# Nested self-attention on one core: zeroes for V from GpSimd, and a 64-row projection order for the 448-row pair

## The chip, the cores and the metric

The kernel runs on one core of a Trainium2 chip. The metric is the device time of one execution, in microseconds (us). Three runs of the kernel before gave 341.05, 342.54 and 338.79 us, a median of 341.05. The engines are written as in the profile: PE (TensorE matmul), PEld (TensorE weight load), DVE (VectorE), ACT (ScalarE), POOL (GpSimd), SP (SyncE).

## What is computed

Thirty-two sequences of up to 512 rows and 512 columns (8 heads of 64) go through a fused projection and softmax attention; each sequence uses only its first `lengths[b]` rows, and all other output rows are zero.

```
for b in range(batch):
    x_b = x[b, :lengths[b]]
    q, k, v = split(x_b @ w_qkv)            # 8 heads of 64 each
    attn = softmax(q @ k.T / sqrt(64))      # per head
    output[b, :lengths[b]] = attn @ v
```

The draw is fixed. Sorted by length, the sequences are worked in 16 pairs, and each pair has a class N, its longer length rounded up to a multiple of 32 (340 is one more class):

| pair | lengths | class | tiles of 128 rows |
|---|---|---|---|
| 0 | 502, 447 | 512 | 4 |
| 1 | 446, 436 | 448 | 4 |
| 2, 3, 4 | 363, 357; 351, 347; 343, 333 | 384, 352, 352 | 3 |
| 5, 6, 7 | 323, 315; 310, 261; 260, 257 | 340, 320, 288 | 3 |
| 8, 9, 10 | 246, 230; 223, 220; 216, 183 | 256, 224, 224 | 2 |
| 11, 12, 13 | 164, 152; 143, 140; 134, 119 | 192, 160, 160 | 2 |
| 14, 15 | 101, 86; 79, 75 | 128, 96 | 1 |

## The kernel before

The program holds, for each class, one straight piece of code per engine and jumps between the pieces by the class read at run time (graph, L1140). A piece has two halves, h = 0 and h = 1, one per sequence of the pair. Half h does the attention of sequence h while it projects Q, K and V of the next sequence, g = 1 - h, whose width W is N, or the next lower class where the pair is the last of its class (leave, L1100). Tensors are doubled by h: xT (transposed input), qkT, v_aug (V with a 65th column of ones per head) and onat (output).

The order on PE is written by hand as a string of tokens (ORDER, L671, and DENSE, L676), read in half (L682):

- S: scores of one head pair for one key tile, two matmuls of 64 contraction rows, into s0 or s1; ACT takes the exponential into ep (L346) and so frees the bank. For dense classes (3 tiles, N up to 340) D does a whole head pair.
- Q, K: a projection of one head pair, four matmuls of 128 rows. Lower case gives its copy to ACT (L409), upper case to DVE (L410). E begins Q and K of a head pair at once in two banks, as eight matmuls of 64 rows; F, G, H or I ends them in eight more, and says which engine copies which bank (G: the first DVE, the second ACT). U and W do the same for two tiles of V.
- V: one tile of V, copied with the row mask by DVE (L433). If the last tile has at most 64 rows (half_rows, L510: W of 288, 320, 160, 192), vsides (L515) computes its two column halves on two halves of the partitions; DVE then writes the low columns (L529), clears the upper partitions of the high columns (L530) and writes their lower partitions (L531).
- A: probabilities times V, 65 columns a matmul; DVE takes the reciprocal (L610) and multiplies into onat (L629, L631). A leading + spreads A's matmuls between those of the step before it (spread_last, L655).
- O: ACT issues the store of the first half of onat; SP stores the second.

Banks: three-tile classes go through four banks in turns (a0, a1 in pa; v0, v1 in pav; in_turns, L842), and an A takes one bank. Two- and four-tile classes alternate a0 and a1 for projections, and A takes pav whole.

POOL's loop (L1699) waits in each half for s_vf, which the first score matmuls of the half raise when v_aug of g may be overwritten; it writes the column of ones (L1652, raising s_on), waits for s_x16f, and casts the input of a later sequence to 16 bit (L1647), after which SP issues the next load and, in the following half, the transposes. PE waits for s_on of h before the half's first A (L754; L698 in one-tile halves).

Of the kernel before, what the change touches and what calls it, by code (L numbers as in the profile page):

```python
# [13 lines left out]
P = 128  # L14
NH = 8
HD = 64
NPAIR = 4
# [6 lines left out]
SECOND = {4: 20, 3: AGAIN, 2: 0, 1: None}  # L24
AT_DENSE = 20
FIRST_DENSE = 4
PIECE = 266
PIECE_DENSE = 274
DENSE_ROWS = 340
# [121 lines left out]
def kernel(  # L151
# [363 lines left out]
    def vsides(pr, b, h, t):  # L515

        n = D // 2
        mms = [
            mm(area[b][HD * a : HD * (a + 1), 0:n], xT[h][:, c, t * P : t * P + HD],
               w_r[:, c, 2 * D + a * n : 2 * D + (a + 1) * n], c == 0, c == NC - 1)  # L520
            for c in range(NC)
            for a in range(2)
        ]

        def evac(e):
            keep = now[0][:, 0, t : t + 1].unsqueeze(2)
            low, high = v_aug[h][:, t, 0:NPAIR, 0:HD], v_aug[h][:, t, NPAIR:NH, 0:HD]
            src = area[b][:, 0:n].rearrange("p (a d) -> p a d", d=HD)
            e.tensor_tensor(out=low, in0=src, in1=keep.broadcast_to([P, NPAIR, HD]), op=ALU.mult)  # L529
            e.memset(high[HD:P], 0.0)  # L530
            return e.tensor_tensor(  # L531
                out=high[0:HD], in0=src[HD:P],
                in1=keep[0:HD].broadcast_to([HD, NPAIR, HD]), op=ALU.mult,
            )

        acquire(pr, b)
        close(pr, b, "dve", mms, True)
        evacuate(pr, b, "dve", evac)
# [5 lines left out]
            return  # L544
        group(pr, b, "dve", v_mms(b, h, i, T, of), v_out(b, h, i, T, of))

    def attnv(pr, h, i, T, late=False, b=None):

        for s_ in ("s0", "s1"):
            if pr.pair[s_] == i or T == 1 and pr.pair[s_] is not None:  # L550
                acquire(pr, s_)
        for v in halves_av if b is None else (b,):
            acquire(pr, v)
        va = v_aug[h]
        if b is not None:
            jobs = [(2 * 74 * qt, i, qt) for qt in range(T)]
        elif T == 1:
            jobs = [(74 * 2 * j, j, 0) for j in range(NPAIR)]
        elif T == 4:
            jobs = [(256 * qt, i, qt) for qt in range(T)]  # L560
        else:
            jobs = [(74 * (4 * qt + 2 * (i % 2)), i, qt) for qt in range(T)]
        mms = []
        for o0, j, qt in jobs:
            for par in range(2):
                o = o0 + par * (HD + 1 if T == 4 else 74)
                into = pav if b is None else area[b]
                for kt in range(T):
                    mms.append(
                        mm(  # L570
                            into[:, o : o + HD + 1],
                            ep[:, j, par, kt, qt * P : (qt + 1) * P],
                            va[:, kt, 2 * j + par, :],
                            kt == 0,
                            kt == T - 1,
                        )
                    )
        if b is None and T in (2, 3) and i % 2 == 0:
            acquire_carry(pr, mms)
            return  # L580
        on = onat[h]
        if b is not None:
            res = into[:, 0 : 2 * 74 * T].rearrange("p (t a d) -> p t a d", a=2, d=74)
            dst = on[:, i // 2, 0:T, P * (i % 2) : P * (i % 2 + 1)]
            dst = dst.rearrange("p t (a d) -> p t a d", d=HD)
            sh, fin = [T, 2], i % 2 == 1
        elif T == 4:
            res = pav.rearrange("p (j n) -> p j n", n=256)[:, :, 0 : 2 * (HD + 1)]
            res = res.rearrange("p j (a d) -> p j a d", d=HD + 1)
            dst = on[:, i // 2, :, P * (i % 2) : P * (i % 2 + 1)]  # L590
            dst = dst.rearrange("p t (a d) -> p t a d", d=HD)
            sh, fin = [NT, 2], i % 2 == 1
        else:
            sh, fin = [2, 4] if T == 1 else [T, 4], True
            res = pav[:, 0 : 74 * sh[0] * 4].rearrange("p (b j d) -> p b j d", j=4, d=74)
            if T == 1:
                dst = on[:, :, 0, :].rearrange("p b (j d) -> p b j d", d=HD)
            else:
                dst = on[:, i // 2, 0:T, :].rearrange("p t (a d) -> p t a d", d=HD)
        rv = rcp[:, i, 0 : sh[0] * sh[1]].rearrange("p (j a) -> p j a", a=sh[1])  # L600
        num, den = res[..., 0:HD], res[..., HD]
        name = "av" if b is None else b
        close(pr, name, "dve", mms, False)
        each = T == 4 or b is not None

        def recip():
            for j in (0, 1) if T == 1 else (i // 2,) if not each or i % 2 == 0 else ():
                pr.take("dve", s_od[h][j], 16)
            pr.take("dve", full[(name, "dve")])
            pr.add("dve", lambda e: e.reciprocal(out=rv, in_=den).then_inc(s_r, 1))  # L610

        def mult():
            pr.take("dve", s_r)

            if T == 1:
                cuts = [(slice(0, 2), 0)]
            elif h == 0:
                cuts = [(slice(0, T - 1), None), (slice(T - 1, T), T - 1)]
            else:
# [26 lines left out]
        if not late:  # L646
            for fn in todo.values():
                fn()
        return todo
# [25 lines left out]
    }  # L675
    DENSE = "K2 q2 D E1 E3 I1 H3 D k0 c A0 Q0~ A1 D V2 O V1 A2 D A3~ V0"  # L676

    def read_class(pr, h):
        for g in ("act", "dve") if h == 0 else ("pe",):
# [2 lines left out]
    def half(pr, h, T, N, W, st, last=False):  # L682
# [11 lines left out]
        if T == 1:  # L694
            start_proj()
            qk(pr, "a0", g, [(i, 0) for i in range(NPAIR)], W, P)
            qk(pr, "a1", g, [(i, 1) for i in range(NPAIR)], W, P, "act")
            pr.take("pe", s_on[h])  # L698
            attnv(pr, h, 0, 1)
            vwhole(pr, g)  # L700
            read_class(pr, h)
            for b in ("a0", "a1"):
                acquire(pr, b)
            pr.signals.append(s_xtf[g])
            if last:
                act_store(pr, h, 0, T)
            scores(pr, h, g, 0, 0, 1, W)
# [2 lines left out]
            return  # L710
        per = T if T >= 3 else 1
        units = [(i, k) for i in (1, 2, 3, 0) for k in range(per)]
        first, norm, dones, both = True, {}, 0, []
        dense, turns = is_dense(N), in_turns(N)
        toks = (DENSE if dense else ORDER[T]).split()

        def pick(second=False):
            if turns:
# [11 lines left out]
        for tok in toks:  # L730
# [16 lines left out]
            elif k == "D":  # L747
                i = units[0][0]
                del units[:T]
                scores_dense(pr, *((g, i, W) if i == 0 else (h, i, N)))  # L750
            elif k == "A":
                if first:
                    first = False
                    pr.take("pe", s_on[h])  # L754
                b = pick(over2) if turns else None
                if turns:
                    assert len(st["seen"]) == len(area), st["seen"]
                    for v in area:
                        if st["holds"].get(v) == (h, "V"):
                            acquire(pr, v)  # L760
                norm[i] = attnv(pr, h, i, T, f"X{i}" in toks, b)
                if turns:
                    give(b)
                if over:
# [5 lines left out]
            else:  # L770
# [26 lines left out]
                else:  # L797
                    bs = (pick(over2),)
                if k == "V":
                    vtile(pr, bs[0], g, i, tiles, T, W)  # L800
                elif k in "Bb":
                    qk(pr, bs[0], g, [(i, 0), (i, 1)], W, 256, eng)
# [37 lines left out]
        return -(-N // P) == 3 and 3 * N <= 2 * MAXS  # L840

    def in_turns(N):  # L842
        return -(-N // P) == 3 and (not is_dense(N) or "E" in DENSE)

    def make_body(N, W, last=False):

# [44 lines left out]
    def make_prologue():  # L891
# [143 lines left out]
        for tok in "Q2 K2 S0 S1 Q3 K3 V0 S2 S3 V1 X2 V2 X3 V3".split():  # L1035
# [23 lines left out]
                cast_second(3)  # L1059
            bank ^= 1  # L1060
        pr.add("dve", mask_table)
        return pr

    def class_table(e):
# [75 lines left out]
    def graph(e, name, opening=None, before=None):  # L1140
# [13 lines left out]
        def align(N, slots, off=0):  # L1154
# [2 lines left out]
                slot = AT_DENSE  # L1157
            elif slots is FIRST and is_dense(N):
                slot = FIRST_DENSE
            if fetch and slot is not None:  # L1160
                e.addr_align(FETCH, offset=(slot + off) % FETCH, max_nops=0)

# [158 lines left out]
    with nc.Block() as block:  # L1321
# [295 lines left out]
        def _(e):  # L1617
# [30 lines left out]
                    s_xc[h], 1  # L1648
                )

            def ones(h, T, src):
                e.tensor_copy(  # L1652
                    out=v_aug[h][:, 0:T, :, HD],
                    in_=src[:, 0, 0:T].unsqueeze(2).broadcast_to([P, T, NH]),
# [44 lines left out]
            def body(e, N):  # L1699
                T = -(-N // P)  # L1700
                for h in range(2):
                    wait_dec(e, s_vf[1 - h])
                    rv = e.snap(rank, min_val=0, max_val=B - 1)
                    ones(1 - h, T, masks[:, bass.ds(rv, 1), :, :].rearrange(
                        "p o a t -> p (o a) t"))
                    wait_dec(e, s_x16f[1 - h])
                    cast(1 - h, T)
                    if T == 1:
# [104 lines left out]
```

## Time and profile before

| | |
|---|---|
| runs | 338.79, 341.05, 342.54 us |
| profiled execution | 339.78 us |
| its span, first to last instruction | 338.0 us |
| granted TensorE clock | 0.996 |
| pair of class 448 | from 63.41 to 99.67 us |
| twelve 3-tile halves | from there to about 237 us |
| twelve 2-tile halves | about 237 to 316 us |

A group row reads: line, engine, operation, output<-input, shapes, count | busy us, mean ns of one | idle time before, and what ended it. A timeline row reads: start, us, engine, line, operation, count, and in brackets the idle time before it with its releaser. A row of several instructions covers them from the first start to the last end; matmul ends are modelled, so the step from one start to the next is the better measure of what PE spends. A wait row reads: engine, what waited, for what, us in total, times, longest (one kind has two engine rows, PE and PEld). L59 is the semaphore take and L304 the matmul helper, so PE's rows are told apart by their tiles.

### The profile page before, as it was taken

What the parts mean: (1) busy time and instruction counts of PE and PEld (TensorE: products, weight loads), DVE (VectorE), ACT (ScalarE), POOL (GpSimd) and SP (SyncE); (2) the same over time, 40 slices, a digit from 0 to 9 for tenths busy, and PEclk for the clock granted to TensorE, in tenths of its full rate; (3) what the DMA queues carried; (4) which work ended last, traced back from release to release, by engine and by line L of the source; (5) the groups of instructions that cost most, each with busy time, mean ns of one, the idle gap of its engine ahead of it and who ended that gap; (6) DMA issues with size and microseconds to landing.
All of it is one profiled execution on the core that took longest, in us unless ns stands there. A gap on an engine that the chain in (4) does not pass through costs nothing. (4 is left out here: it accounts for less than half of the span.)

```text
span 338.0 us, 12174 instructions
## 1 busy us (share of the span) xinstructions
PE 324.0 (96%) x4326; PEld 207.2 (61%) x4327; DVE 215.3 (64%) x580; ACT 240.0 (71%) x337; POOL 63.2 (19%) x102
## 2 busy tenths in 40 slices
PE   7899999999999999999999999999999999999991
PEld 2565544555545656556666676777677777676770
DVE  3576566666665576567567556765767667777672
ACT  4567887777769878877977887778775666555541
POOL 3634020202010210220220122012111211221340
PEclk9999999999999999999999999999999999999998
DMA  6956799966856976986787978697899657886732
GB/s 203 360 145 215 131 395 243 355 155 214 163 183 153 299 263 162 282 294 183 233 305 247 225 237 298 137 260 218 209 148 240 189 148 170 200 166 154 174 105 69
DMA packets 82273, 72.11 MB, mean 213 GB/s; under 512 B 40652, under 2 KB 63180, under 8 KB 82196
## 3 DMA queue, kind: packets, MB, share of 16 engines
q1 hardware_dynamic: 70340, 59.61, 66.7%
q10 hardware_dynamic: 11856, 11.54, 9.8%
q8 instruction: 40, 0.66, 0.8%
q14 instruction: 37, 0.30, 0.4%
HBM read 25.32 MB, written 36.70 MB: 183 GB/s over the span
## 5 line engine op out<-in xcount | busy, mean ns | idle before, releaser
L346 ACT ACTIVATE ep<-psc 128x704 f16<-128x704 f32 (+7 forms) x193 | 156.8, 858 | 60.2 <-PE psc L304 42.9
L304 PE MATMUL pa<-xT,w_r 128*128 128x224 f16 (+21 forms) x984 | 134.0, 276 | 3.0 <-PEq L59 1.3
L304 PEld LDWEIGHTS pa<-xT,w_r 128*128 128x128 f16 (+1 forms) x984 | 74.7, 97 | 35.5 <-issue 14.1
L410 DVE CAST qkT<-pa 128x448 f16<-128x448 f32 (+9 forms) x85 | 48.7, 574 | 47.1 <-PE pa L304 46.0
L304 PE MATMUL psc<-qkT 64*128 64x352 f16 (+17 forms) x702 | 66.9, 287 | 0.9 <-PEq L59 0.3
L304 PE MATMUL pa<-w_r,xT 128*128 128x512 f16 (+4 forms) x356 | 63.4, 333 | 0.6 <-DVE v_aug L531 0.5
L304 PE MATMUL pav<-v_aug,ep 128*128 128x65 f16 x1414 | 62.1, 194 | 0.2 <-PEq L59 0.2
L304 PEld LDWEIGHTS pav<-v_aug,ep 128*128 128x128 f16 x1414 | 55.4, 98 | 9.7 <-issue 1.4
L1652 POOL CAST v_aug<-masks 128x24 f16 (+4 forms) x33 | 9.1, 276 | 245.4 <-POOLq L1281 245.4
L631 DVE SCALAR_TENSOR_TENSOR onat<-pav,masks,rcp 128x128 f32<-128x128 f32 (+2 forms) x137 | 48.2, 391 | 5.6 <-DVE rcp L610 2.1
L378 ACT ACTIVATE ep<-psc 128x960 f16<-128x960 f32 (+3 forms) x48 | 43.3, 960 | 8.8 <-PE psc L304 6.0
L433 DVE TENSOR_TENSOR v_aug<-pa,masks 128x512 f16<-128x512 f32 (+1 forms) x52 | 34.8, 675 | 14.7 <-PE pa L304 13.8
L304 PE MATMUL pav<-xT,w_r 64*128 64x352 f16 (+10 forms) x328 | 43.6, 300 | 0.3 <-DVE v_aug L433 0.3
L1647 POOL CAST x<-x_nat 128x1536 f16<-128x1536 f32 (+3 forms) x33 | 42.0, 1274 | 9.2 <-POOLq L1281 8.4
L304 PEld LDWEIGHTS psc<-qkT 64*128 64x128 f16 x702 | 25.8, 94 | 29.0 <-issue 20.6
L304 PEld LDWEIGHTS pa<-w_r,xT 128*128 128x128 f16 (+2 forms) x356 | 24.9, 98 | 21.0 <-issue 4.8
L409 ACT CAST qkT<-pa 128x352 f16<-128x352 f32 (+7 forms) x58 | 26.4, 461 | 15.0 <-PE pa L304 8.0
L304 PEld LDWEIGHTS pav<-xT,w_r 64*128 64x128 f16 (+1 forms) x328 | 23.7, 95 | 10.0 <-issue 2.1
L610 DVE RECIPROCAL rcp<-pav 128x8 f32<-128x8 f32 (+1 forms) x71 | 14.0, 198 | 20.4 <-PE pav L304 15.7
L304 PE MATMUL pav<-w_r,xT 128*128 128x512 f16 (+3 forms) x100 | 19.3, 343 | 0.0
L304 PEld LDWEIGHTS pa<-v_aug,ep 128*128 128x128 f16 x378 | 13.5, 98 | 4.3 <-issue 1.8
L629 DVE TENSOR_TENSOR onat<-pav,rcp 128x256 f32<-128x256 f32 (+1 forms) x32 | 14.6, 457 | 1.1
(84 smaller groups left out, 146.4 us busy)
## 6 DMA issues: line engine op xcount, KB each, us to landing
out_dram<-zt SPq DMA_DIRECT2D x16, 768.0 KB, 6.1
x_nat<-in_x_dram SPq DMA_DIRECT2D x12, 512.0 KB
x_nat<-in_x_dram SPq DMA_DIRECT2D x5, 1024.0 KB
out_dram<-onat ACTq DMA_DIRECT2D x12, 384.0 KB, 5.4
out_dram<-onat SPq DMA_DIRECT2D x12, 384.0 KB, 4.7
x_nat<-in_x_dram SPq DMA_DIRECT2D x17, 256.0 KB, 6.3
out_dram<-onat ACTq DMA_DIRECT2D x16, 256.0 KB, 3.8
x_nat<-in_x_dram SPq DMA_DIRECT2D x4, 768.0 KB
```

The lines of the kernel that those rows point to most:

```text
L304: return lambda e: e.matmul(o, lhsT, rhs, start=start, stop=stop)
L346: lambda e: e.activation(out=dst, in_=src, func=AF.Exp, scale=scale),
L378: lambda e, par=par, b=b: e.activation(out=ep[:, i, par, 0:3, 0:N], in_=psc_f[:, par, 0 : 3 * N].rearrange("p (t n) -> p t n", n=N), func= ...
L409: return lambda e: e.copy(out=dst, in_=src)
L410: return lambda e: e.tensor_copy(out=dst, in_=src)
L433: return lambda e: e.tensor_tensor(out=v_aug[h][:, t, lo // HD : lo // HD + n, 0:HD], in0=area[b][:, 0:w].rearrange("p (a d) -> p a d", d=HD),
L610: pr.add("dve", lambda e: e.reciprocal(out=rv, in_=den).then_inc(s_r, 1))
L629: ins = e.tensor_tensor(op=ALU.mult, **ops)
L631: ins = e.scalar_tensor_tensor(scalar=now[0][:, 1, t : t + 1], op0=ALU.mult, op1=ALU.mult, **ops)
L1647: e.tensor_copy(out=x16[h][:, 0:T, :], in_=x_nat[h][:, 0:T, :]).then_inc(s_xc[h], 1)
L1652: e.tensor_copy(out=v_aug[h][:, 0:T, :, HD], in_=src[:, 0, 0:T].unsqueeze(2).broadcast_to([P, T, NH]),).then_inc(s_on[h], 1)
```

## The change

- DVE's clear in vsides goes away. In its place POOL clears all 128 partitions of the high columns of the last tile, ahead of the ones, in every two- and three-tile half.
- PE's wait for s_on moves: from before the first A, for the sequence attended, to before the last tile's V, for the sequence projected (in one-tile halves to before the scores; one take more at the end of the prologue).
- Classes 448 and 416 use four banks in turns and a new order, FOUR. A covers query tiles 0 and 1 and the new Z covers tiles 2 and 3, each in one bank; Q and K are all projected in 64-row halves with copies split between DVE and ACT. The alignment offset of PE's code for these classes becomes 4 instead of 20.

```
+FOUR_ROWS = 448
+AT_FOUR = 4
...
-            e.memset(high[HD:P], 0.0)
...
-    def attnv(pr, h, i, T, late=False, b=None):
+    def attnv(pr, h, i, T, late=False, b=None, qts=None):
...
-            jobs = [(2 * 74 * qt, i, qt) for qt in range(T)]
+            jobs = [(2 * 74 * k, i, qt) for k, qt in enumerate(qts)]
...
-            sh, fin = [T, 2], i % 2 == 1
+            sh, fin = [n, 2], i % 2 == 1 and T - 1 in qts
...
+            elif b is not None:
+                whole = [] if h else [k for k, t in enumerate(qts) if t < T - 1]
+                cuts = [(slice(0, len(whole)), None)] if whole else []
+                cuts += [(slice(k, k + 1), t) for k, t in enumerate(qts) if k not in whole]
...
+    FOUR = "S E1 S G1 S E2 S G2 S E0 S E3 S G0 G3 S S A0 Z0 V1 +A1 S S Z1 V3 +A2 S O S V0 +Z2 S A3 Z3 S S V2"
...
-            pr.take("pe", s_on[h])
             attnv(pr, h, 0, 1)
...
+            pr.take("pe", s_on[g])
             if last:
...
-        toks = (DENSE if dense else ORDER[T]).split()
+        toks = (DENSE if dense else FOUR if T == 4 and turns else ORDER[T]).split()
...
-            elif k == "A":
-                if first:
-                    first = False
-                    pr.take("pe", s_on[h])
+            elif k in "AZ":
...
-                norm[i] = attnv(pr, h, i, T, f"X{i}" in toks, b)
+                cut = 2 if T == 4 and turns else T
+                qts = range(cut) if k == "A" else range(cut, T)
+                norm[i] = attnv(pr, h, i, T, f"X{i}" in toks, b, qts)
...
                 if k == "V":
+                    if i == T - 1:
+                        pr.take("pe", s_on[g])
                     vtile(pr, bs[0], g, i, tiles, T, W)
...
-        return -(-N // P) == 3 and (not is_dense(N) or "E" in DENSE)
+        return 2 * P < N <= FOUR_ROWS
...
+            elif 3 * P < N <= FOUR_ROWS:
+                slot = AT_FOUR
...
-            def ones(h, T, src):
+            def ones(h, T, src, clear=False):
+                if clear:
+                    e.memset(v_aug[h][:, T - 1, NPAIR:NH, 0:HD], 0.0)
...
-                    "p o a t -> p (o a) t"))
+                    "p o a t -> p (o a) t"), T in (2, 3))
```

The old order for four tiles, which classes 512 and 480 keep, is `S S Q0 +A0 S S K0 V0 S S Q1 +A1 S S K1 V1 S S Q2 +A2 S S K2 V2 S S Q3 +A3 S S V3 K3 O`.

More of the change, by code (lines that the diff above doesn't have):

```diff
@@ L565, in attnv @@
             for par in range(2):
-                o = o0 + par * (HD + 1 if T == 4 else 74)
+                o = o0 + par * (HD + 1 if T == 4 and b is None else 74)
                 into = pav if b is None else area[b]
@@ L582, in attnv @@
         if b is not None:
-            res = into[:, 0 : 2 * 74 * T].rearrange("p (t a d) -> p t a d", a=2, d=74)
-            dst = on[:, i // 2, 0:T, P * (i % 2) : P * (i % 2 + 1)]
+            n = len(qts)
+            res = into[:, 0 : 2 * 74 * n].rearrange("p (t a d) -> p t a d", a=2, d=74)
+            dst = on[:, i // 2, qts[0] : qts[0] + n, P * (i % 2) : P * (i % 2 + 1)]
             dst = dst.rearrange("p t (a d) -> p t a d", d=HD)
-            sh, fin = [T, 2], i % 2 == 1
+            sh, fin = [n, 2], i % 2 == 1 and T - 1 in qts
         elif T == 4:
@@ L599, in attnv @@
                 dst = on[:, i // 2, 0:T, :].rearrange("p t (a d) -> p t a d", d=HD)
-        rv = rcp[:, i, 0 : sh[0] * sh[1]].rearrange("p (j a) -> p j a", a=sh[1])
+        r0 = 2 * qts[0] if b is not None else 0
+        rv = rcp[:, i, r0 : r0 + sh[0] * sh[1]].rearrange("p (j a) -> p j a", a=sh[1])
         num, den = res[..., 0:HD], res[..., HD]
@@ L606, in recip @@
         def recip():
-            for j in (0, 1) if T == 1 else (i // 2,) if not each or i % 2 == 0 else ():
+            opens = i % 2 == 0 and (b is None or 0 in qts)
+            for j in (0, 1) if T == 1 else (i // 2,) if not each or opens else ():
                 pr.take("dve", s_od[h][j], 16)
@@ L712, in half @@
         units = [(i, k) for i in (1, 2, 3, 0) for k in range(per)]
-        first, norm, dones, both = True, {}, 0, []
+        norm, dones, both = {}, 0, []
         dense, turns = is_dense(N), in_turns(N)
-        toks = (DENSE if dense else ORDER[T]).split()
+        toks = (DENSE if dense else FOUR if T == 4 and turns else ORDER[T]).split()
         def pick(second=False):
@@ L1061, in make_prologue @@
         pr.add("dve", mask_table)
+        pr.take("pe", s_on[0])
         return pr
```

## Prediction

> **What bounds the kernel now.** I read the page's engine line first, then the waits, then the PE timeline of the two places that the change touches, with DVE and ACT beside them.
>
> ```profile
> PE 324.0 (96%) x4326; PEld 207.2 (61%) x4327; DVE 215.3 (64%) x580; ACT 240.0 (71%) x337; POOL 63.2 (19%) x102
> ```
>
> PE is busy for 324.0 of 338.0 us; no other engine is near. An edit pays only where PE stands still or streams less. The whole program's waits:
>
> ```profile
> PE pa L304 <- DVE v_aug L531: 0.5, 3, 0.2
> PEld psc L304 <- ACT ep L346: 1.7, 6, 0.3
> ACT ep L346 <- PE psc L304: 42.9, 64, 1.5
> POOL v_aug L1652 <- POOLq L1281: 245.4, 31, 16.6
> ```
>
> PE waits three times for line 531, the instruction behind the clear that the change takes off DVE. PE's loads wait only six times for an exponential, while ACT waits 64 times for scores. POOL spends 245.4 us waiting for s_vf. So the whole stake is some 14 us of PE idle time and the gaps inside PE's busy time, and the change reaches a few of them.
>
> **Part 1: the clear moves from DVE to POOL.** Ten runs leave DVE; 24 come to POOL (the twelve 3-tile and twelve 2-tile halves, half rows or not).
>
> ```profile
> L530 DVE MEMSET v_aug<- 64x256 f16 x10 | 2.7, 272 | 0.9
> L1658 POOL MEMSET ep<- 128x1024 f32 x6 | 5.4, 955 | 7.9 <-DVE x L950 7.9
> L140 POOL MEMSET ident_f<- 128x128 f32 x1 | 0.2, 194 | 0.0
> ```
>
> A POOL clear of 256 elements lies between 0.19 us (128 elements) and 0.96 us (1024); on the line between them it takes 0.30 us, and that is the value I take, because 256 is nearest to 128. That adds 24 x 0.30 = 7.2 us, covered by the 245.4 us of waiting. What DVE's 10 x 0.272 = 2.7 us are worth depends on who waits. Six lie in 2-tile halves, where V1 (with the clear) is followed by A3 and then by V0, which needs V1's bank. PE first, then DVE, then POOL:
>
> ```profile
> 273.65 0.65 PE L304 MATMUL pav<-v_aug,ep 128*128 128x65 f16 x16
> 274.14 1.03 PE L304 MATMUL pa<-w_r,xT 128*128 128x512 f16 x4
> 278.63 0.63 PE L304 MATMUL pa<-w_r,xT 128*64 128x256 f16 x8
> 280.12 0.65 PE L304 MATMUL pav<-v_aug,ep 128*128 128x65 f16 x16
> 280.79 1.02 PE L304 MATMUL pa<-w_r,xT 128*128 128x512 f16 x4
> 286.50 0.65 PE L304 MATMUL pav<-v_aug,ep 128*128 128x65 f16 x16
> 287.31 1.04 PE L304 MATMUL pa<-w_r,xT 128*128 128x512 f16 x4 [0.16 <-DVE v_aug L531]
> ```
> ```profile
> 286.83 0.43 DVE L531 TENSOR_TENSOR v_aug<-pa,masks 64x256 f16<-64x256 f32 x1
> ```
> ```profile
> 275.66 0.26 POOL L1652 CAST v_aug<-masks 128x16 f16 x1 [5.46 <-POOLq L1281]
> ```
>
> Sixteen A3 matmuls take 274.14 - 273.65 = 0.49 us when V0 need not wait. In the h=1 half it is 280.79 - 280.12 = 0.67, a loss of 0.18; in the h=0 half 287.31 - 286.50 = 0.81, a loss of 0.32, and 286.83 + 0.43 = 287.26 shows line 531 ending just before V0 starts. A DVE chain shorter by 0.272 and one hand-over gives back at most about 0.29. Classes 224 (second half), 192 and 160 make three losses of each kind: 3 x 0.18 + 3 x 0.29 = 1.4 us. The other four clears lie in dense 3-tile halves, where DVE works without a break up to V0's copy, whose bank the next half's first cross projection takes:
>
> ```profile
> 197.28 0.58 PE L304 MATMUL psc<-qkT 64*128 64x320 f16 x8
> 197.84 0.72 PE L304 MATMUL pav<-xT,w_r 64*128 64x320 f16 x8
> 208.44 0.58 PE L304 MATMUL psc<-qkT 64*128 64x320 f16 x8
> 208.86 0.28 PE L304 MATMUL pav<-xT,w_r 64*128 64x288 f16 x1
> 220.16 0.67 PE L304 MATMUL pav<-xT,w_r 64*128 64x288 f16 x8 [0.30 <-DVE v_aug L433]
> ```
> ```profile
> 219.33 0.69 DVE L433 TENSOR_TENSOR v_aug<-pav,masks 128x512 f16<-128x512 f32 x1
> ```
>
> Eight scores of 320 columns need 208.86 - 208.44 = 0.42 us; ahead of 197.84 they take 0.56, a loss of 0.14, and 220.16 shows 0.30. Behind the even halves nothing is lost. That is 0.14 + 0.29 = 0.4 us. Part 1 together: 1.8 us. From both sides: 2.7 if all ten lay on PE's path, 0 if another wait steps in. I take 1.8, since each piece has its row. What is late next is the scores' bank, which ACT frees; ACT is the one that waits there (64 times), so I count nothing.
>
> The new wait stands ahead of the last V instead of the half's first A: as many waits as before, no more. Behind it on PE's queue is everything that follows. In the 2-tile half POOL's ones start at 275.66 and V1 at 278.63; with 0.30 + 0.26 the signal falls near 276.3, with a 0.96 clear near 276.9, so 1.7 to 2.3 us of cover remain; in 3- and 4-tile halves the last V lies later still. Without the cover, each of 24 halves would pay what is missing. Behind the clear on POOL the cast, and then SP's next load, go out up to 0.3 us later; the transposes that need the cast belong to the following half (halves are 286.50 - 280.12 = 6.4 us apart here). Cost 0; if that slack were gone, 0.3 us per half.
>
> **Part 2: the pair of class 448** (rows 446 and 436), the only pair that the new order reaches; class 416 does not occur. PE's steps there, then the same kinds of step in the 3-tile pair behind it:
>
> ```profile
> 63.41 0.55 PE L304 MATMUL psc<-qkT 64*128 64x448 f16 x4
> 64.08 0.35 PE L304 MATMUL pa<-xT,w_r 128*128 128x448 f16 x1
> 65.90 0.55 PE L304 MATMUL psc<-qkT 64*128 64x448 f16 x4
> 66.39 0.93 PE L304 MATMUL pa<-xT,w_r 128*128 128x448 f16 x4
> 67.16 1.03 PE L304 MATMUL pa<-w_r,xT 128*128 128x512 f16 x4
> 99.67 0.82 PE L304 MATMUL pa<-xT,w_r 128*128 128x384 f16 x4 [0.30 <-DVE v_aug L433]
> 103.94 0.73 PE L304 MATMUL pa<-v_aug,ep 128*128 128x65 f16 x18
> 104.51 0.71 PE L304 MATMUL pav<-v_aug,ep 128*128 128x65 f16 x18
> 105.15 0.34 PE L304 MATMUL psc<-qkT 64*128 64x384 f16 x2
> 113.94 0.76 PE L304 MATMUL pa<-xT,w_r 64*128 64x352 f16 x8
> 114.53 0.33 PE L304 MATMUL psc<-qkT 64*128 64x384 f16 x2
> 114.69 0.76 PE L304 MATMUL pav<-xT,w_r 64*128 64x352 f16 x8
> ```
>
> The two halves last 99.67 - 63.41 = 36.26 us, 0.30 of it the wait at 99.67.
> - Row-size switches. A score step of two streams 114.69 - 114.53 = 0.16 us at 384 columns, 0.187 at 448. Two of them last 66.39 - 65.90 = 0.49, so leaving 64-row work costs 0.49 - 0.37 = 0.12. Eighteen A matmuls take 0.57 (104.51 - 103.94); 105.15 - 104.51 = 0.64 shows 0.07 for entering it. The old order has eight such islands per half, the new one five: 3 x 0.19 = 0.57 saved.
> - Projections. A 64-row set of eight takes 114.53 - 113.94 = 0.59 at 352 columns, 0.75 at 448; four 128-row matmuls take 67.16 - 66.39 = 0.77. Eight per half: 0.15 saved.
> - A and Z. Eighty of 128 matmuls no longer have a projection between them. Between projections one takes (65.90 - 64.08 - 0.77 - 0.07)/32 = 0.031 us, alone 0.57/18 = 0.032, or 0.49/16 = 0.031 above: 0 to 0.08 in all. I take 0.05.
>
> So 0.57 + 0.15 - 0.05 = 0.67 per half, 1.3 for both, if nothing waits. What waits:
>
> ```profile
> 62.95 0.68 DVE L433 TENSOR_TENSOR v_aug<-pa,masks 128x512 f16<-128x512 f32 x1
> 63.63 0.66 DVE L410 CAST qkT<-pa 128x480 f16<-128x480 f32 x1
> ```
> ```profile
> 66.31 1.73 ACT L346 ACTIVATE ep<-psc 128x896 f16<-128x896 f32 x2 [0.70 <-PE psc L304]
> 270.37 0.53 ACT L409 CAST qkT<-pa 128x448 f16<-128x448 f32 x1
> ```
>
> - The start. E1 takes both pa banks, Q0 took one. The second is freed by the last K copy at 63.63 + 0.66 = 64.29; E1 could stream from 63.41 + 0.19 = 63.60. That is 0.7 us of waiting, against about 0.2 us that the old start lost (64.08 instead of 63.41 + 0.49 = 63.90): costs 0.5.
> - The end. The 0.30 us at 99.67 is k3 waiting for V3's copy; in the new order bank a0 is long free there: saves 0.3.
> - ACT. Two scores and a G give ACT 1.73 + 0.53 = 2.26 us of work while PE streams 2 x (0.187 + 0.75) = 1.87. Over four G's ACT falls back by 1.5 us at most; the two score buffers absorb about one step (0.94), so between 0 and 0.6 us per half comes through. I take 0.2, since the 3-tile halves interleave in this manner and the six waits above average 0.3: costs 0.4.
> - DVE gets one reciprocal and at most one product more per head pair. I cost them at nothing, since PE streams at least one other set of matmuls before the bank that they free is used again; if that cover were gone, each is below line 531's 0.43 us, so 4 x 2 x 0.43 = 3.4 us per half at most.
>
> Part 2: 1.3 - 0.5 + 0.3 - 0.4 = 0.7 us saved.
>
> **Sum.** 339.78 us (the profiled execution; 338.0 of it span) - 1.8 - 0.7 = 337.3 us, which is 0.7% less. The median of the runs shown, 341.05, lies 1.3 above this execution, and they spread over 3.8; on the median the same saving reads 338.6, so the range reaches up by 1.3 more than the mechanisms ask.
>
> **Rivals.**
> 1. ACT paces the 448 pair (other side). If copies and exponentials do not overlap and each G's bank comes free only behind two exponentials, E0 and E3 stand as well: the whole 1.5 us, plus a copy of 0.53 and its bank's hand-over, some 2.2 us per half. Part 2 becomes 1.3 - 0.5 + 0.3 - 4.4 = a loss of 3.3, and the sum 339.78 - 1.8 + 3.3 = 341.3. From 1.45 us of wait per half on, the change as a whole loses. For it: ACT's 2.26 against 1.87. Against it: ACT waits for PE in the old order far more than PE for ACT. Chance 0.14.
> 2. The clears' time is not given back, because the next copy on DVE or ACT ends as late: 339.78 - 0.7 = 339.1. Against it: line 531 is named at the wait. Chance 0.12.
> 3. A POOL clear holds DVE up while it runs, so that DVE loses 0.30 in the chain of the dense halves and again in the six 2-tile chains: 11 x 0.3 = 3.3 at most, of which perhaps 1.5 on PE's path: 337.3 + 1.5 = 338.8.
>
> ```profile
> 219.44 1.47 POOL L1647 CAST x<-x_nat 128x1536 f16<-128x1536 f32 x1
> ```
>
> This cast runs over the DVE copy of 219.33, which takes its usual 0.69 us (0.68 at 62.95). Chance 0.10. [...]
> 4. More comes back: the start's wait and ACT's are hidden (part 2 gives 1.3 + 0.3 + 0.2 = 1.8) and all ten clears count (2.7): 335.3. Chance 0.18.
>
> My forecast has the remaining 0.46. **Range:** 335.3 to 341.3, from rival 4 to rival 1, with the 1.3 of the median inside; the forecast's own cases span 336.5 to 338.3. **Chances.** A measurement of this kernel can tell about 1% (3.4 us) from no change. Faster by over 1% asks for less than 336.4: rival 4 and a little of the forecast, 0.23. Slower by over 1% asks for more than 343.2: the tail of rival 1, and PE's code for this class, whose alignment offset goes from 20 to 4, which no row prices: 0.07. Within 1%: 0.70.
>
> **What would show it.** Line 530 is gone, 24 POOL clears near 0.3 us stand ahead of the ones, and no PE row names line 531. A3 to V0 takes 0.49 to 0.53 in the six 2-tile halves. In the 448 pair the first projection starts near 64.35, its two halves last about 35.6 us together, and the first 3-tile projection follows without a gap. Wrong would be: PE rows that wait for ACT with more than 1 us per half, POOL's signal later than the last V, or equal A3 to V0 times.

## The result, and the profile after

The kernel after takes 338.79 us (median of 22 runs, 337.59 to 340.50), the kernel before 340.60 us (22 runs, 338.46 to 343.28). The ratio is 0.9938, 95% interval 0.9920 to 0.9957: about 0.6% less, under the 1% that counts as a difference here. The prediction was 337.3 against the profiled execution's 339.78: 2.5 us of gain forecast, where the medians show 1.8. The interval reaches from 1.5 to 2.7 us, so the runs alone do not tell 2.5 from 2.0; the stages of the traces have to. The profiled execution after took 338.92 us, span 337.2, granted clock 0.994.

The page's engine line after:

```profile
PE 321.1 (95%) x4390; PEld 207.9 (62%) x4391; DVE 209.9 (62%) x578; ACT 243.0 (72%) x345; POOL 67.8 (20%) x126
```

DVE has lost 5.4 us, POOL has gained 4.6, PE streams 2.9 us less. The new clear as a group of the page:

```profile
L1666 POOL MEMSET v_aug<- 128x256 f16 x24 | 7.5, 314 | 187.5 <-POOLq L1294 187.5
```

The 24 clears take 0.314 us each (I took 0.30), all in POOL's waiting time. Of the waits after, these three answer to those shown of before:

```profile
PE pa L306 <- PEq L61: 3.4, 6, 2.0
PEld psc L306 <- ACT ep L348: 2.1, 7, 0.4
PEld pa L306 <- DVE v_aug L435: 1.8, 4, 0.9
```

No PE row names DVE's writes of the column halves (now L531 and L532) any more. Loads waiting for exponentials have hardly grown (1.7 to 2.1 us). Loads waiting for V's whole-tile copy (L435, before L433) have grown from 1.2 to 1.8 us: 0.9 of it is E1's first load in the 448 pair, the other three waits are at the projection b1 of 2-tile halves. One wait of 2.0 us for a semaphore is new. The last two are what the experiments are about. Now the places that the prediction named, on PE's timeline after: the start and end of the 448 pair, two dense places, then two 2-tile halves.

```profile
62.33 0.36 PE L306 MATMUL psc<-qkT 64*128 64x448 f16 x2
63.35 0.93 PE L306 MATMUL pa<-xT,w_r 64*128 64x448 f16 x8 [0.66 <-DVE qkT L412]
64.11 0.37 PE L306 MATMUL psc<-qkT 64*128 64x448 f16 x2
98.10 0.81 PE L306 MATMUL pa<-xT,w_r 128*128 128x384 f16 x4
...
195.66 0.58 PE L306 MATMUL psc<-qkT 64*128 64x320 f16 x8
196.08 0.71 PE L306 MATMUL pav<-xT,w_r 64*128 64x320 f16 x8
217.56 0.54 PE L306 MATMUL psc<-qkT 64*128 64x288 f16 x8
218.13 0.67 PE L306 MATMUL pav<-xT,w_r 64*128 64x288 f16 x8
...
278.10 0.65 PE L306 MATMUL pav<-v_aug,ep 128*128 128x65 f16 x16
278.58 1.03 PE L306 MATMUL pa<-w_r,xT 128*128 128x512 f16 x4
279.98 1.79 PE L306 MATMUL pa<-xT,w_r 128*128 128x192 f16 x16
281.60 0.66 PE L306 MATMUL pav<-v_aug,ep 128*128 128x65 f16 x16
284.55 0.65 PE L306 MATMUL pav<-v_aug,ep 128*128 128x65 f16 x16
285.04 1.03 PE L306 MATMUL pa<-w_r,xT 128*128 128x512 f16 x4
287.55 0.65 PE L306 MATMUL pav<-v_aug,ep 128*128 128x65 f16 x16
```

- The 448 pair lasts 98.10 - 62.33 = 35.77 us, before 36.26. E1 waits 0.66 us for the last K copy, and k3 waits for nothing.
- Dense: 196.08 - 195.66 = 0.42 (before 0.56), and 218.13 - 217.56 = 0.57 where before had 220.16 - 219.32 = 0.84. Together 0.41 us.
- Two-tile: A3 to V0 is 278.58 - 278.10 = 0.48 and 285.04 - 284.55 = 0.49; all six such halves read 0.48 or 0.49 now.
- But b1 of the half that follows (the second set of the x16 row) has become longer: 281.60 - 279.98 = 1.62 us from B0 to A0. The same rows before, and A0 behind the next half:

```profile
282.23 1.50 PE L304 MATMUL pa<-xT,w_r 128*128 128x192 f16 x16
283.56 0.66 PE L304 MATMUL pav<-v_aug,ep 128*128 128x65 f16 x16
...
289.84 0.65 PE L304 MATMUL pav<-v_aug,ep 128*128 128x65 f16 x16
```

There it was 283.56 - 282.23 = 1.33. So 0.29 us was lost again here. In the two like places of classes 160, counted from the scores ahead of B0 to A0, it was 0.18 (1.80 against 1.62) and 0.17 (1.81 against 1.64). DVE after, beside these rows, and PE's load for b1:

```profile
278.90 0.21 DVE L614 RECIPROCAL rcp<-pav 128x8 f32<-128x8 f32 x1 [0.65 <-DVEq L61]
279.40 0.88 DVE L639 SCALAR_TENSOR_TENSOR onat<-pav,masks,rcp 128x256 f32<-128x256 f32 x2 [0.30 <-DVEq L61]
280.19 0.68 DVE L435 TENSOR_TENSOR v_aug<-pa,masks 128x512 f16<-128x512 f32 x1
280.85 0.56 DVE L412 CAST qkT<-pa 128x384 f16<-128x384 f32 x1
280.93 0.61 PEld L306 LDWEIGHTS pa<-xT,w_r 128*128 128x128 f16 x8 [0.34 <-DVE v_aug L435]
```

V0 ends about 279.6 on PE, but its copy starts at 280.19, behind A3's reciprocal and products, and ends at 280.87. b1 needs that copy's bank (a1, as the two banks alternate), and B0's eight matmuls are through at about 279.98 + 0.66 = 280.64. b1's load names that copy as what it waited for, here and in the two like places.

### The profile page after: what moved, and what is told of

It reads as the page before. It is cut to its first block, busy times and chain, and to the rows that moved or that the text cites. A ratio compares the mean times of both kernels' runs of the same rounds, so it can differ in the third digit from the quotient of the medians.

```text
span 337.2 us, 12374 instructions
## 1 busy us (share of the span) xinstructions
PE 321.1 (95%) x4390; PEld 207.9 (62%) x4391; DVE 209.9 (62%) x578; ACT 243.0 (72%) x345; POOL 67.8 (20%) x126
## 5 line engine op out<-in xcount | busy, mean ns | idle before, releaser
L306 PE MATMUL pa<-xT,w_r 128*128 128x224 f16 (+21 forms) x984 | 122.9, 275 | 5.0 <-PEq L61 3.4
L412 DVE CAST qkT<-pa 128x512 f16<-128x512 f32 (+9 forms) x73 | 41.5, 570 | 45.5 <-PE pa L306 42.6
L306 PE MATMUL pav<-v_aug,ep 128*128 128x65 f16 x1254 | 55.0, 194 | 0.4 <-PEq L61 0.4
L306 PEld LDWEIGHTS pav<-v_aug,ep 128*128 128x128 f16 x1254 | 49.0, 98 | 9.0 <-issue 1.6
L306 PE MATMUL pav<-xT,w_r 64*128 64x352 f16 (+12 forms) x392 | 50.8, 307 | 0.0
L1666 POOL MEMSET v_aug<- 128x256 f16 x24 | 7.5, 314 | 187.5 <-POOLq L1294 187.5
L411 ACT CAST qkT<-pa 128x352 f16<-128x352 f32 (+8 forms) x62 | 28.7, 468 | 15.6 <-ACTq L61 7.8
L435 DVE TENSOR_TENSOR v_aug<-pa,masks 128x512 f16<-128x512 f32 (+1 forms) x46 | 30.7, 672 | 13.8 <-PE pa L306 13.5
L614 DVE RECIPROCAL rcp<-pav 128x8 f32<-128x8 f32 (+2 forms) x69 | 13.5, 196 | 22.5 <-PE pav L306 16.6
L306 PE MATMUL pav<-w_r,xT 128*128 128x512 f16 (+3 forms) x124 | 26.9, 350 | 0.0
L306 PE MATMUL pa<-v_aug,ep 128*128 128x65 f16 x538 | 22.3, 194 | 0.0
```

What stands on the lines that cost most here:

```text
L306: return lambda e: e.matmul(o, lhsT, rhs, start=start, stop=stop)
L411: return lambda e: e.copy(out=dst, in_=src)
L412: return lambda e: e.tensor_copy(out=dst, in_=src)
L435: return lambda e: e.tensor_tensor(out=v_aug[h][:, t, lo // HD : lo // HD + n, 0:HD], in0=area[b][:, 0:w].rearrange("p (a d) -> p a d", d=HD),
L1666: e.memset(v_aug[h][:, T - 1, NPAIR:NH, 0:HD], 0.0)
```

## The experiments

**Theory.** The clears' gain is cut where V0's copy stands behind A3's norm on DVE; the rest of the gain is on PE's path as forecast. **Rivals.** The new 2.0 us wait gives the gain back late in the program; or the clears are worth nothing and all of it comes from the order of the 448 pair or from the moved wait. "448" is the time from the pair's first scores to the first 3-tile projection, "2-tile" from the first scores of 224 columns to the first of 128 columns, "1-tile" from there to the last scores, each in that run's one profile. Each ratio is to runs of the kernel before taken together with that kernel, whose medians lay between 340.23 and 340.71 us.

| kernel | median us | ratio to before, interval | 448 | 2-tile | 1-tile |
|---|---|---|---|---|---|
| before | 340.60 | 1 | 36.26 | 64.12 | 12.86 |
| after | 338.79 | 0.9938 (0.9920 to 0.9957) | 35.77 | 63.29 | 14.54 |
| after again | 338.33 | 0.9930 (0.9900 to 0.9960) | 35.76 | 63.19 | 13.42 |
| clears and wait alone | 339.69 | 0.9966 (0.9939 to 0.9993) | 36.10 | 63.02 | 14.52 |
| 448 order alone | 339.09 | 0.9950 (0.9922 to 0.9977) | 35.76 | 64.29 | 12.48 |
| moved wait alone | 340.03 | 0.9974 (0.9947 to 1.0001) | 36.10 | 64.08 | 13.08 |
| after, dense clears only | 339.54 | 0.9969 (0.9942 to 0.9995) | 35.77 | 64.41 | 13.42 |
| after, other bank order | 337.91 | 0.9923 (0.9888 to 0.9958) | 35.26 | 63.17 | 14.37 |
| the same again | 338.04 | 0.9941 (0.9915 to 0.9966) | 35.13 | 63.17 | 12.68 |
| after, one load | 338.77 | 0.9941 (0.9914 to 0.9968) | 35.75 | 63.28 | 14.32 |
| after, copy first | 341.64 | 1.0028 (0.9999 to 1.0056) | 35.77 | 66.81 | 13.23 |
| after, V0 ahead of A3 | 340.88 | 1.0019 (0.9993 to 1.0045) | 35.75 | 66.01 | 12.97 |
| V0 ahead, other bank order | 340.35 | 0.9999 (0.9970 to 1.0028) | 35.11 | 66.02 | 12.95 |
| before, register moves | 340.39 | 1.0001 (0.9974 to 1.0028) | 36.25 | 64.11 | 13.62 |

### The parts by themselves

Clears and moved wait without the new order:

```
-FOUR_ROWS = 448
-            toks = (DENSE if dense else FOUR if T == 4 and turns else ORDER[T]).split()
+            toks = (DENSE if dense else ORDER[T]).split()
...
-        return 2 * P < N <= FOUR_ROWS
+        return -(-N // P) == 3 and (not is_dense(N) or "E" in DENSE)
```

> Part 1 alone: POOL's clear and the moved wait, the order for class 448 as before. My theory: DVE's clear was on PE's path in the dense halves (0.4 us, all of it back) and in the 2-tile halves (1.4 us of waiting ahead of V0), but in the 2-tile halves part of it is only handed on: V0's copy still stands behind A3's products on DVE, so that B0's partner b1 in the next half waits for it instead. I expect 1.2 to 1.5 us faster than before (ratio 0.996). Rival (everything comes back, as the prediction had it): 1.8 us or more. Rival (clears hidden): 0 to 0.3 us.

Measured 339.69, ratio 0.9966: 1.0 us below before (by the interval 0.2 to 2.1). The runs do not tell the expected 1.2 to 1.5 from its rivals; the 2-tile stage, 1.1 us shorter than before and as short as in after, does. This profile also has a wait of 1.10 us for a semaphore ahead of the first projection of class 256, which no other profile has, so its 3-tile stage is longer than before's.

The new order with the clear on DVE and the wait where it was:

```
+            e.memset(high[HD:P], 0.0)
...
+                if first:
+                    first = False
+                    pr.take("pe", s_on[h])
...
-                    if i == T - 1:
-                        pr.take("pe", s_on[g])
```

> Part 2 alone: the new order for class 448 with DVE's clears and the old waits. My theory: the 448 pair shrinks by 0.5 us as in the changed kernel (36.26 to 35.8), the 2-tile halves stay as before; 0.3 to 0.7 us faster (ratio 0.9985). Rival (ACT paces the pair): the pair is no shorter, 0 or slower. If both parts add up, this and the clear alone give together the 2 us of the whole change.

Measured 339.09, ratio 0.9950. The pair takes 35.76 us, a gain of 0.50 in the trace. The runs say more (by the ratio 1.7 us, interval 0.8 to 2.7), and the profile shows it at no one place: no other stage is more than 0.4 us shorter than before. What the runs have beyond 0.5 us stays unexplained. The two parts make 2.7 us together in the medians, more than the whole change, within these intervals. The new alignment offset came with the order in every run; what it does alone no run shows.

The kernel before with the moved wait alone:

```
-                if first:
-                    first = False
-                    pr.take("pe", s_on[h])
...
+                    if i == T - 1:
+                        pr.take("pe", s_on[g])
```

> Only PE's wait for the ones moves to the last V; DVE keeps its clear and POOL gets none. My theory: the wait itself costs nothing and gives little: the first half of the program, where the first projection takes five waits, may start 0.2 us earlier; 0 to 0.3 us faster, the 2-tile halves as before. Rival (the moved wait is the gain, not the clear): over 1 us faster, as much as with the clear.

Measured 340.03, ratio 0.9974, interval up to 1.0001. The trace has 0.16 us in the 448 pair (36.10) and 0.15 in the pair of class 512, both ahead of the first projection of a half; the rest is within the spread. I had costed this edit at nothing. In the 448 pair it does not add to the new order's gain: with the old wait the new order's pair takes 35.76 us, with the moved one 35.77.

The clear on POOL in three-tile halves only:

```
+            if t == 1:
+                e.memset(high[HD:P], 0.0)
...
-                        "p o a t -> p (o a) t"), T in (2, 3))
+                        "p o a t -> p (o a) t"), T == 3)
```

> Kernel after, but GpSimd clears only in three-tile halves; in two-tile halves the memset is on DVE again as before. Theory transfers (the two-tile gain is given back at the first one-tile half, where the staged transpose comes no earlier): the two-tile halves get about 0.8 us longer, the wait of 1.5 to 2.0 us before the first projection of the second one-tile half goes away or shrinks by as much, and the time is that of after within 0.3 us, perhaps below. Theory TensorE (the two-tile gain counts in full, the wait is chance): 0.8 us slower than after, ratio to before about 0.996.

Measured 339.54 us, 0.9 us above after (34 runs of after in two sets, median 338.63; interval of the difference 0.4 to 1.7). PE of this kernel, A3 and V0 of an h = 0 half:

```profile
286.98 0.65 PE L306 MATMUL pav<-v_aug,ep 128*128 128x65 f16 x16
287.78 1.04 PE L306 MATMUL pa<-w_r,xT 128*128 128x512 f16 x4 [0.16 <-DVE v_aug L534]
```

287.78 - 286.98 = 0.80: the old loss is back in all six halves, and the 2-tile stage takes 64.41. The 2-tile clears are worth 0.9 us in the runs, as the stage says from before to after (64.1 to 63.2). This kernel's 64.41 is 0.3 above before: in the h = 1 half of class 192 A3's reciprocal starts 1.15 us behind A3 in place of 0.80, and b1 waits there though V0 comes no earlier; no row names why. The theory that the gain is given back by the new wait falls: it had expected the time of after within 0.3 us.

### What is late next in the two-tile halves

V0's copy ahead of A3's norm on DVE, with a release of A3's banks of its own behind the products:

```
-        2: "S S B0 b1 A0 A1 B2 S S V1 b3 A2 O A3 R3 X3 V0",
+        2: "S S B0 b1 A0 A1 B2 S S V1 b3 A2 O A3 V0 R3 X3",
```

> Kernel after with one edit: in two-tile halves V0's copy stands ahead of A3's reciprocal and products on DVE. Theory copy (b1 of a half waits for bank a1, which V0's copy frees, and that copy stands behind A3's norm): the 0.2 to 0.3 us waits before b1 vanish, b1 to its A0 falls from 1.62, 1.42 and 1.81 us to about 1.3, and the halves give back up to 0.6 us; A0 of the next half may then wait for A3's products, which come some 0.7 us later. Theory transfers (SP's chain, not TensorE, sets when the first one-tile half can go on: in the three profiles with the clears on GpSimd TensorE waits 1.5 to 2.0 us there, in the three without it does not): the halves get shorter, the wait there longer by as much, and the time stays at that of after. Rival (b1 waits for something else): no change at b1.

It is 3.0 us slower than after. PE and DVE of this kernel at the place shown above:

```profile
281.72 1.49 PE L306 MATMUL pa<-xT,w_r 128*128 128x192 f16 x16
283.59 0.65 PE L306 MATMUL pav<-v_aug,ep 128*128 128x65 f16 x16 [0.38 <-PEq L61]
```
```profile
281.59 0.69 DVE L435 TENSOR_TENSOR v_aug<-pa,masks 128x512 f16<-128x512 f32 x1 [1.41 <-DVEq L61]
...
282.54 0.88 DVE L639 SCALAR_TENSOR_TENSOR onat<-pav,masks,rcp 128x256 f32<-128x256 f32 x2
283.35 0.55 DVE L412 CAST qkT<-pa 128x384 f16<-128x384 f32 x1
```

The x16 row is 1.49 us again, as before the change (1.50): b1 does not wait, so it was V0's copy that it waited for. But DVE now stands idle for 1.41 us until V0 is projected, the products end at 283.4, and A0 waits 0.38 us for them. The theory is right and the remedy wrong.

So V0 was put ahead of A3 on PE as well, so that its copy runs while A3 does:

```
+        2: "S S B0 b1 A0 A1 B2 S S V1 b3 A2 O V0 A3 R3 X3",
```

> Kernel after with V0's projection and its copy ahead of A3 in two-tile halves (O V0 A3 R3 X3), and a release of A3's banks behind its products. Theory copy (what took back part of the clears' gain is V0's copy standing behind A3's reciprocal and products): now the copy runs while A3 does, so the 0.2 to 0.3 us before b1 go without the 0.4 to 0.5 us before A0 that the copy alone ahead of the products cost: halves of about 5.8 us in place of 6.02 to 6.07, and 0.6 to 1.2 us less than after. Rival (the three two-tile pairs are paced by another thing, the exponentials on ACT or the release of A3's banks): A0 or V0 waits as long as b1 did, and the time is that of after within 0.3 us or above it.

340.88 us, 2.3 above after: the forecast of 0.6 to 1.2 less is wrong, the rival right. PE of this kernel:

```profile
278.85 0.41 PE L306 MATMUL pav<-v_aug,ep 128*128 128x65 f16 x8
279.50 1.02 PE L306 MATMUL pa<-w_r,xT 128*128 128x512 f16 x4 [0.25 <-PEq L61]
280.36 0.41 PE L306 MATMUL pav<-v_aug,ep 128*128 128x65 f16 x8
...
281.14 1.49 PE L306 MATMUL pa<-xT,w_r 128*128 128x192 f16 x16
282.76 0.65 PE L306 MATMUL pav<-v_aug,ep 128*128 128x65 f16 x16
```

Only b3 and A2's eight matmuls stand between V1 and V0 now, no longer A3's, so V0 waits 0.25 us for V1's copies; and A0 still comes 1.62 us behind B0, because DVE again does the copy first and the products behind it. In after A2 and A3, sixteen matmuls, cover V1's copies, and the norm ahead of the copy keeps A0 from waiting; the order of after is the best of the three, and its price is b1's 0.2 to 0.3 us.

### The start of the 448 pair

The banks in another order, so that E1 does not need a1, whose copy is the last of the pair before:

```
+        if T == 4 and turns:
+            st["banks"] = ["a0", "v0", "a1", "v1"]
```

> The changed kernel with the four banks of class 448 taken in the order a0, v0, a1, v1, so that the first E1 no longer needs the bank of the last K copy of the pair before. My theory: the 0.66 us that PE stands ahead of E1 goes to 0.1 or less and 0.4 to 0.6 us come off the changed kernel (2.4 to 2.7 us faster than before). Rival (ACT paces the pair, so the wait only moves to a later score): the pair takes the same 35.8 us.

> The kernel with the other order of the four banks once more, for a second profile and more times. The start of the 448-row pair is 0.7 us shorter than in after at its first projection, as in the first profile (1.04 us from the first scores to the second in place of 1.78): that must be seen again; whether the staged transpose of the first one-tile half is waited for again is open. Time: 0.7 us below after.

In both profiles the second scores follow the first in 1.04 us in place of 1.78: E1's wait, the 0.5 us of the prediction's start, is gone, and the pair takes 35.26 and 35.13 us. That is 0.51 and 0.64 less than after, not 0.74: two loads of scores now wait for exponentials (0.17 and 0.24 us in the second profile), and the steps there are 0.21 and 0.08 us longer in all. The two sets (22 runs, median 338.00) lie 0.6 us below after, interval 1.2 below to 0.2 above; the gain is in both traces, the runs alone leave it unclear. Together with V0 ahead of A3:

> The last kernel and the four banks of the 448-row pair in the other order (a0, v0, a1, v1) together. If both gains lie on TensorE's path and at different places they add: about 0.5 us (the start of the 448-row pair) below the last kernel, ratio to before about 0.989 to 0.990. If the two-tile halves give nothing, 0.992.

340.35 us, 0.5 below the kernel with V0 ahead alone (interval 1.5 below to 0.5 above), with the same 35.11 and 66.02 in its stages: the two places are independent, and the second loses.

### The new wait in the one-tile halves

After has a wait that before had not. PE's first projection of the second one-tile half needs xT, which POOL copies into place once SP's staged transpose has landed. The timeline after, all engines:

```profile
315.66 0.38 ACTq L1302 DMA_DIRECT2D out_dram<-onat  x1
...
315.76 1.23 SPq L1513 DMA_TRANSPOSE xT<-x  x1
...
320.65 0.61 POOL L1710 COPY xT<-xT 128x512 f16<-128x512 f16 x1 [3.27 <-POOLq L1294]
...
321.40 1.52 PE L306 MATMUL pa<-xT,w_r 128*128 128x96 f16 x32 [1.96 <-PEq L61]
```

The transpose is issued 0.10 us behind ACT's 256 KB store, and the copy starts 320.65 - 315.76 = 4.89 us after it. The same of before:

```profile
317.47 1.19 SPq L1500 DMA_TRANSPOSE xT<-x  x1
...
318.30 0.38 ACTq L1289 DMA_DIRECT2D out_dram<-onat  x1
...
320.36 0.61 POOL L1695 COPY xT<-xT 128x512 f16<-128x512 f16 x1 [0.19 <-POOLq L1281]
```

There it is issued 0.83 us ahead of the store, and the copy starts after 2.89 us. Is it SP's chain, which comes later against a faster TensorE? One load instead of two:

```
-                    load(1 - h, 5, N, index(h, 0))
+                    load(1 - h, 5, 2 * P, index(h, 0))
...
-                    lambda: load(1 - h, 5, N, index(h, 0)),
+                    lambda: load(1 - h, 5, 2 * P if T == 2 else N, index(h, 0)),
```

> Kernel after with one edit: in two-tile halves SP loads the next tokens with one DMA of 256 rows in place of one of 128 and one of the rest (the added rows are not used), about 0.55 us less of SP's time in each half. Theory transfers (SP's chain through the two-tile halves is as long as TensorE's and sets the first one-tile half's transpose): SP's transposes fall back behind TensorE less, the wait there shrinks from 1.5 to 2.0 us towards 0, and the time falls 0.5 to 1.7 us below after. Theory TensorE: the time of after within 0.3 us, the wait as it comes by chance.

338.77 us, the time of after, and the wait is there with 1.78 us: SP's load is not what sets it. And after again:

> Kernel after without an edit, as the measure for the other three and for a second profile. Theory transfers: the wait of 1.5 to 2.0 us at the first one-tile half is there again, and the start of the 512-row stage, set by loads, may differ by some tenths. Theory TensorE (chance): any wait from 0 to 2 us. Time: 0.994 of before.

338.33 us, and its profile has no wait at that place: transpose issued 0.17 us ahead of the store, copy after 3.91 us. So one kernel shows both; the second run of the other bank order lacks the wait as well (1.50 us in the first). To bring it about on purpose, SP's transpose in the kernel before was to be delayed:

```
+                    if h == 0:
+                        for _ in range(16):
+                            e.reg_mov(tmp, 0)
```

> The kernel before with one edit: SP executes 16 register moves ahead of the staged transpose of the first of two one-tile halves, which delays it by some tenths to 1 us and so lets ACT's 256 KB store be issued ahead of it, as in after. Theory collision (in the profiles so far the transpose lands 2.9 to 3.6 us after its issue where it is issued 0.6 us or more ahead of ACT's store, and 4.5 to 5.1 us where it is issued with it or behind it; that and not the delay itself makes TensorE wait): it lands 4.5 us or more after its issue, and TensorE waits 0.5 to 2 us before the first projection of the second one-tile half, where before had no wait; the time is 0.5 to 2 us above before. Rival (the long landings were chance, or come from the shorter two-tile halves): it lands in 2.9 to 3.6 us, the delay stays within the 1.2 us that TensorE has in hand there, and the time is that of before.

The edit did nothing, and the delay that was expected of it rested on no measurement: from the end of the store on SP to the transpose are 1.57 us, against 1.56 in before and after, and its page counts 12174 instructions, as many as the page of before. It is one more execution of before (ratio 1.0001), and by chance it has the wait (its timeline, all engines):

```profile
317.78 1.21 SPq L1504 DMA_TRANSPOSE xT<-x  x1
317.85 0.40 ACTq L1289 DMA_DIRECT2D out_dram<-onat  x1
...
322.25 0.61 POOL L1699 COPY xT<-xT 128x512 f16<-128x512 f16 x1 [2.54 <-POOLq L1281]
...
323.01 1.52 PE L304 MATMUL pa<-xT,w_r 128*128 128x96 f16 x32 [0.85 <-PEq L59]
```

Issued 0.07 us ahead of the store, copy after 4.47 us, wait 0.85. Over all 14 profiles: nine with the transpose 0.17 us or more ahead of the store, copy after 2.88 to 3.91 us, no wait there; five with it at most 0.08 us ahead, or 0.08 to 0.26 behind, 4.47 to 5.06 us and a wait of 0.85 to 1.96. That the store beside the transpose makes it late fits every profile, but no run set it on purpose. Four of the five belong to the six profiles with the shorter 2-tile stage, one to the old stage; whether the change makes the wait more frequent stays open. In the medians it does not undo the 2-tile gain, as the kernel with the dense clears only shows.

## Why the prediction was right, and where it was off

- **Size.** 2.5 us forecast. By the traces: 0.41 (dense) + 0.9 (2-tile) + 0.5 (448 pair) + 0.15 (the 512 pair) = 2.0; by the medians 1.8, and 2.0 with the second set of after. The moved wait's 0.15, which the prediction did not have, makes up for a part of what it had too large; to that extent the sum is nearer than its terms by luck.
- **POOL's clear: right.** 0.314 us against 0.30, hidden; no PE row waits for the ones.
- **Dense, 0.43: right.** 0.41 at the two places named.
- **Two-tile, 1.4: the mis-sized term.** A3 to V0 gave back all that was forecast, 3 x 0.19 + 3 x 0.32 = 1.5 us. The step that failed is "What is late next is the scores' bank, which ACT frees ... so I count nothing". What was late next is V0's own copy on DVE: V0 comes earlier, but A3's norm does not end earlier, and b1, or B0 with it, pays 0.29 + 0.18 + 0.17 = 0.64. Net 0.9. It splits by halves. In the h = 1 halves A3 to A0 takes 281.60 - 278.10 = 3.50 where before had 283.56 - 280.12 = 3.44, and in classes 160 3.25 and 3.26 where before had 3.25 twice: nothing was kept there. (In class 192, 0.14 of b1's loss is A3's products starting 0.50 us behind the reciprocal in place of 0.36; no row names why.) In the h = 0 halves it takes 287.55 - 284.55 = 3.00 where before had 289.84 - 286.50 = 3.34, and the two like places gain 0.28 and 0.34: there V0's copy starts 1.17 or 1.18 us behind V0 in both kernels, so it follows V0 and the gain stays. The rows for it were in the trace of before (DVE, the same place):

```profile
281.28 0.88 DVE L631 SCALAR_TENSOR_TENSOR onat<-pav,masks,rcp 128x256 f32<-128x256 f32 x2
282.07 0.68 DVE L433 TENSOR_TENSOR v_aug<-pa,masks 128x512 f16<-128x512 f32 x1
```

The copy starts right behind the products there too, in an h = 1 half, so they bound it already, and V0 could only come nearer to them.
- **448 pair, 0.7: nearly right.** 0.49 came. The start cost what was said: 0.74 us gross against 0.7, shown by the other bank order. The end's 0.30 is gone. Now without the waits: before is 36.26 - 0.30 - 0.18 (what the old start lost, 64.08 - 63.90) = 35.78, after is 35.77 - 0.74 = 35.03. That is 0.75, where switches, projections and ACT's share had made 0.9. ACT does not pace the pair, but it takes some 0.1 to 0.2 us back once E1's wait is gone (the other bank order).
- **The moved wait, 0:** 0.15 us by the traces, in the pair of class 512. Alone it gives 0.16 in the 448 pair as well, but that is the loss of the old start, which the prediction had set against E1's wait and which the new order removes by itself.
- **Rival 1** (ACT paces) falls: the pair is shorter, and loads waiting for exponentials rose by 0.4 us in the whole program. **Rival 2** (the time is not given back, because the next copy ends as late) is right in kind for 0.64 of the 1.5 us, and wholly so in the h = 1 halves; it was given 0.12 as a whole. **Rival 4** falls by the size.
- **Rival 3** (POOL's clear holds DVE up) falls. A clear beside DVE's chain of above, and the group of those products:

```profile
280.05 0.31 POOL L1666 MEMSET v_aug<- 128x256 f16 x1 [4.93 <-POOLq L1294]
```
```profile
L639 DVE SCALAR_TENSOR_TENSOR onat<-pav,masks,rcp 128x256 f32<-128x256 f32 x36 | 16.2, 478 | 2.0 <-DVE rcp L614 1.0 <-DVEq L61 0.3
```

The clear runs from 280.05 to 280.36, over the end of the products at 279.40 and the start of the copy at 280.19; these take 0.88 and 0.68 us as without it, and the 36 products average 478 ns in both kernels.

## What to carry to other kernels

When a wait is taken away, look at what frees the bank after the next one: if that copy already starts right behind another instruction of its engine, it is the next wait, and the gain ends there: here in three of six halves, wholly. A shorter DVE queue did not help here where the copy stands behind work which another engine's result starts (V0's copy behind A3's norm: in class 192 A3 to A0 took 3.50 us after, 3.44 before). And when an order looks improvable, count what each matmul set covers: moving V0 by one place uncovered 0.25 us at one end and moved 0.3 us at the other.

## What the runs showed of the hardware

- In these 14 profiles the copy that needs a staged transpose of one tile starts 4.47 to 5.06 us after the transpose's issue where another queue's 256 KB store is issued at most 0.08 us behind the transpose, or ahead of it, and 2.88 to 3.91 us after it where the store comes 0.17 us or more behind. No run set this on purpose; that the store is what delays the copy is not shown.
- The time from the kernel's start to the 448 pair differs by 1.17 us between two profiles of the same kernel after (62.33 and 63.50 us to its first scores); DVE waits 0.9 us for the first loads in one and 2.0 in the other. The two profiled executions of the other bank order took 337.74 and 335.87 us: 1.87 us apart, more than the 1.8 us that the medians give the change. The 448 and 2-tile stages repeat within 0.13 us where a kernel was profiled twice (before and the register moves, after, the other bank order); the 3-tile stage of before differs by 0.3 and the 1-tile stages by up to 1.7.
